# Hybrid attention/Hyena block: the filters' second small layer in fixed places among the first half's block cycles, and a late part's sums closed in one PSUM bank

## The chip, the cores and the metric

One core of one Trainium2 chip runs the whole kernel as one program. The metric is device time in microseconds for one execution. The kernel before was timed three times: 1696.48, 1691.30 and 1693.38 us, median 1693.38 us. A fourth execution was recorded by the hardware profiler: its own time is 1691.19 us and its span, from the first recorded instruction to the last, is 1689.4 us. All positions in time below are microseconds from the start of that span.

Engine names as the profile has them: PE is the matrix engine (matmuls and transposes), DVE the vector engine, ACT the scalar engine (activation functions, copies, casts), POOL the general engine, which here issues transfers, and SP the engine whose queue issues most loads. Each engine runs its own instructions in the order in which they stand.

## What is computed

One trunk layer over 1024 latent tokens and 256 context tokens of width 1024. Only the part that bears on the change is shown:

```
mod   = silu(c)     @ w_ada + b_ada        # 6 parts of 1024: shift1 scale1 gate1 shift2 scale2 gate2
mod_c = silu(c_ctx) @ w_ada + b_ada
h  = rmsnorm(x, norm1_g)   * (1 + scale1)  + shift1
hc = rmsnorm(ctx, norm1_g) * (1 + cscale1) + cshift1
k_c, v_c = split(hc @ w_in[:, 512:1536])
q, k, v, hv, hx1, hx2, gna, ghy = split(h @ w_in)

# Hyena filters: a small network of a position t, two sine layers of width 64
hid  = sin(freq * (features(t) @ w1 + b1))
hid  = sin(freq * (hid @ w2 + b2))
filt = (hid @ w3) * exp(-t * deltas)
```

After that come neighbourhood attention, a two-step long convolution with `filt`, a gated merge, and a SwiGLU feed-forward stage modulated by shift2, scale2 and gate2.

## The kernel before

**Tiles and stages.** Activations are kept with channels on the 128 partitions, so 1024 channels are 8 blocks (k = 0 to 7), and tokens run along the free axis in two halves of 512 (context: 256). A product of float32 accuracy is made of three fp32r matmuls: each operand is split into a high part (an ACT cast, line 177) and a low part (a DVE subtraction, line 178), and low x high, high x low and high x high are summed.

**The opening stage** is the one that the change touches, roughly the first 113 us of the span. `project` and its `opening` (line 792) multiply the normalized, modulated tokens by the value columns of `w_in`: for the first half of the tokens, then the second, then the context, and in each for k = 0 to 7. The operands of block k come from the generator `hidden`, which `opening` advances with `next(between)`. In the first half, block k's cycle also makes modulation block k + 1: eight small matmuls into a bank `ada_ps` (line 233), an ACT copy `msb`, four tiny matmuls that turn it into columns (line 244), two DVE operations that write `mod1` (lines 245 and 247); then ACT makes `htmp` from the transposed tokens `hT_ps` with it, casts it to `hTh`, and DVE makes `hTl`. In the second half and for the context the modulation is there already, and a cycle is: the transposes of block k + 2 on PE (line 261), `htmp` and `hTh` on ACT, `hTl` on DVE (`hcTh`, `hcTl` for the context), and then on PE eight matmuls that need `hTh` and a last four that need `hTl`.

**Side work in the opening.** Two more generators are advanced at fixed points of `hidden`:

- `filter_hidden` (`mlp`) makes the two sine layers. Each layer is two PE matmuls of 512 columns (line 453, bank `mlp_ps`), two DVE operations that add the bias and multiply by freq (line 454), five DVE operations of 1024 columns that bring the argument into the range of the sine (lines 455 to 463), and one ACT sine (line 465) that writes `feat` for the first layer and `hid` for the second. The sine needs a table of its own, which ACT loads ahead of it.
- `wide_sums` (`sums`) makes two late parts of the modulation, parts 3 and 4, by multiply-and-add on DVE: sixteen steps i = 0 to 15, each with one loaded row block `wal` of 128x1024 (line 1096 for the first step of a part, 1093 for the others). Step i issues load i + 3, so three loads are ahead. After the steps of a part `total` adds over the partitions with matmuls by a matrix of ones (line 1054, bank `ar_ps`) and DVE adds the sums to a row tile `arow` (line 1057).

**What sets the order.** Most instructions of this stage are pinned (`keep_in_program_order`): they stand on their engine as the generators produced them. Those that are not pinned are placed by the scheduler of the tile framework. Buffers come from pools: PSUM banks with the tag `f` (five of them) carry `ada_ps`, `hT_ps`, `mlp_ps` and `ar_ps` in turn; a ring of eight 128x1024 SBUF buffers carries in turn the raw weights, the x and context rows, the `wal` loads and the accumulator `aacc`. An instruction that writes a buffer waits until the last reader of its earlier content is done.

In the kernel before, the second sine layer is produced in the second half: its two matmuls on PE and its seven argument operations on DVE stand together in the cycle of block 6, after the closing of part 3. The sine itself stands on ACT ahead of `htmp` of block 7.

Of the kernel before, what the change touches and what calls it, by code (L numbers as in the profile page):

```python
# [10 lines left out]
F32 = mybir.dt.float32  # L11
F32R = mybir.dt.float32r
AF = mybir.ActivationFunctionType
ALU = mybir.AluOpType
# [4 lines left out]
P = 128  # L19
# [141 lines left out]
class Block:  # L161
# [121 lines left out]
    def hidden(self, pool, wpool, h1, mp, held, late, hT, hcT, psf):  # L283
# [30 lines left out]
        next(mlp)  # L314
# [26 lines left out]
        def split_weight(k):  # L341
            self.split(*(t[:, k % 2] for t in self.wv[k // 2]), raws[k], inorder)
# [13 lines left out]
        next(mlp)  # L356
# [8 lines left out]
        for k in range(8):  # L365
            h = pool.tile([P, 512], F32, tag="htmp", name="htmp", bufs=3)
# [3 lines left out]
            if k < 3:  # L370
                next(mlp)
# [5 lines left out]
            if k < 7:  # L377
                self.ada_cols_of(*ada, k + 1, sel)
                if 1 <= k + 1 <= 4:
                    block(k + 4)  # L380
                    if k in (0, 2):
                        weight(2 + k // 2)
                    for j in ((), (6, 7), (4,), (5,))[k]:
                        inorder(load(j))
                split_weight(k + 1)
                if 3 <= k:
                    square((6, 7, 4, 5)[k - 3], inorder)
                if k == 5:
                    xs.extend(ring("x") for _ in range(2))
                    for j in (8, 9):  # L390
                        inorder(load(j))
                    sums = self.wide_sums(ring, pool, psf)
                    next(sums)
                if k in (4, 6):
                    r = scaled(10 - k, 2, f"rstd1{k}", inorder)
                    for j in range(2):
                        times(xs[10 - k + j], r[:, j:j + 1], inorder)
# [6 lines left out]
        for k in range(8):  # L404
# [12 lines left out]
            if k in (1, 6):  # L417
                for _ in range(6 if k == 6 else 1):
                    next(mlp)
            if k == 6:  # L420
                after = [self.turned(psf, xs[8:], k, True) for k in range(2)]
# [3 lines left out]
        for k in range(8):  # L425
            if k:
                self.chunk(pool, after[k], 2, self.mod1[:, 1], *hcT, k, None, inorder, True)
            if k < 6:
                after.append(self.turned(psf, xs[8:], k + 2, True))
            if k in (0, 2, 4, 6):  # L430
                next(sums, None)
            yield

    def filter_hidden(self, pool, late, psf):
# [7 lines left out]
        for b in range(2):  # L442
            if b:
                hid, w3 = late()
                nc.sync.dma_start(w3, a["fw3"])
            w, src, dst = (w2, z, hid) if b else (w1, z[0:66], z)
            held = (lambda i: i) if b else pin
            arg = pool.tile([P, T], F32, tag="farg", name="farg", bufs=1)
            kf = pool.tile([P, T], F32, tag="fkf", name="fkf", bufs=1)
            for h in range(2):  # L450
# [3 lines left out]
                held(nc.vector.tensor_scalar(arg[:, sl], ps, col[:, b:b + 1], col[:, 2:3], op0=ALU.add, op1=ALU.mult))  # L454
            held(nc.vector.tensor_scalar(kf, arg, 1.0 / TWO_PI, MAGIC, op0=ALU.mult, op1=ALU.add))
            yield
            held(nc.vector.tensor_scalar(kf, kf, MAGIC, None, op0=ALU.subtract))
            yield
            held(nc.vector.scalar_tensor_tensor(arg, kf, -C1, arg, op0=ALU.mult, op1=ALU.add))
            yield  # L460
            held(nc.vector.scalar_tensor_tensor(arg, kf, -C2, arg, op0=ALU.mult, op1=ALU.add))
            yield
            held(nc.vector.tensor_scalar(arg, arg, PI_LO, -PI_LO, op0=ALU.min, op1=ALU.max))
            yield
            nc.scalar.activation(dst, arg, AF.Sin)
# [600 lines left out]
    def wide_sums(self, ring, pool, psf):  # L1066
# [15 lines left out]
        def total(part, acc):  # L1082
            for h in range(2):
                self.late_total(psf, r, ones, acc[:, 512 * h:512 * h + 512], part - 3, h, pin)
# [609 lines left out]
```

## Time and profile before

| | |
|---|---|
| median of three runs | 1693.38 us |
| profiled execution: own time | 1691.19 us |
| profiled execution: span | 1689.4 us |
| PE busy | 1647.0 us, 97% of the span |
| DVE busy | 1225.4 us, 73% |
| ACT busy | 697.8 us, 41% |
| mean granted PE clock | 0.992 |
| first-half cycle on PE (22.49 to 27.31) | 4.82 us |
| second-half cycle on PE (68.05 to 71.29) | 3.24 us |
| PE idle between 75 and 94 | 4.54 us and 5.99 us |

A row of a timeline gives the start, the length, the engine, the line, the operation with the tile that it writes and those that it reads, the shape and the count; in square brackets stands how long the engine was idle just before, and what ended that. For a load's line in the SP queue, the start is when the transfer was issued. A matmul in plain float32 shows as two records, so `x2` there is one matmul. Rows of a view by windows give, for a stretch of time, the busy time of each engine and, as PEclk, the share of full speed at which PE was clocked.

### The profile page before, as it was taken

Reading aid. Unit: us, or ns where it says so; the run is one execution under the profiler, and the core shown is the slowest. Engines: PE = TensorE matmul, PEld = TensorE weight load, DVE = VectorE, ACT = ScalarE, POOL = GpSimd, SP = SyncE. Lnnn points to the kernel's source line nnn. Section 1 sums busy time; section 2 is a strip of 40 time slices with the busy share of each in tenths; the row PEclk is TensorE's granted clock in tenths of the full one; section 3 lists DMA queues with packets and bytes.
Section 4 is the critical chain, followed back from the end, with each engine's and each line's share of the span. In section 5 each row is a group of like instructions: output and inputs, shape, how many; then the busy total and the mean of one; then the engine's idle time right before and its main releaser. Section 6 shows DMA issues by size and latency. Waiting matters only on the chain.

```text
span 1689.4 us, 22635 instructions
## 1 busy us (share of the span) xinstructions
PE 1647.0 (97%) x8138; PEld 1304.1 (77%) x8138; DVE 1225.4 (73%) x2071; ACT 697.8 (41%) x1216; POOL 148.6 (9%) x272
## 2 busy tenths in 40 slices
PE   8889999999999999999999999999999999999997
PEld 5667777777777788887887887888888888878886
DVE  4757899699999685556765868877865666389467
ACT  6453343312212146455653226633334333355455
POOL 1020000101000050111100001000100111000000
PEclk9999999999999999999999999999999999999999
DMA  9733555554555283445648314333432223395344
GB/s 361 256 133 128 184 174 189 190 173 161 181 201 194 93 265 126 130 122 161 191 157 279 123 63 175 131 129 121 150 106 94 100 103 116 115 384 162 100 120 155
DMA packets 108005, 274.37 MB, mean 162 GB/s; under 512 B 15215, under 2 KB 24307, under 8 KB 105589
## 3 DMA queue, kind: packets, MB, share of 16 engines
q1 hardware_dynamic: 87992, 212.39, 37.6%
q0 software_dynamic: 19104, 60.08, 10.5%
q8 instruction: 65, 1.06, 0.3%
q10 hardware_dynamic: 797, 0.45, 0.1%
q14 instruction: 47, 0.39, 0.1%
HBM read 205.48 MB, written 67.39 MB: 162 GB/s over the span
## 4 chain that ended last, share of the span: by engine, by line
PE 61%; DMA 3%; DVE 2%; issue 1%; ACT 1%; SPq 0%; DVEq 0%; ACTq 0%
PE x_ps L1393 15%; PE in_ps L199 9%; PE z_ps L1393 7%; PE out_ps L1331 5%; PE dx_ps L1562 5%; PE dz_ps L1562 3%; PE hy_ps L199 3%; PE y_ps L1393 2%; PE pt_ps L967 2%; PE pt_ps L953 2%; PE na_ps L199 2%; DMA w<-in_w 1%; PE s_ps L933 1%; PE dy_ps L1562 1%; DMA yhraw<-yh 1%
## 5 line engine op out<-in xcount | busy, mean ns | idle before, releaser
L199 PE MATMUL in_ps<-hTh,wl 128*128 128x512 f32 x576 | 233.0, 405 | 0.5 <-ACT proj L761 0.5
L199 PE MATMUL in_ps<-hTh,wh 128*128 128x512 f32 x576 | 227.3, 395 | 0.0
L199 PE MATMUL in_ps<-hTl,wh 128*128 128x512 f32 x576 | 226.3, 393 | 0.0
L199 PEld LDWEIGHTS in_ps<-hTh,wl 128*128 128x128 f32 x576 | 108.2, 188 | 26.4 <-issue 4.1
L199 PEld LDWEIGHTS in_ps<-hTh,wh 128*128 128x128 f32 x576 | 108.2, 188 | 23.9 <-issue 0.3
L199 PEld LDWEIGHTS in_ps<-hTl,wh 128*128 128x128 f32 x576 | 108.3, 188 | 21.8
L177 ACT CAST wh<-wr 128x1024 fp32r<-128x1024 f32 (+1 forms) x60 | 52.6, 877 | 140.9 <-PE in_ps L199 118.0
L178 DVE TENSOR_TENSOR wl<-wr,wh 128x1024 fp32r<-128x1024 f32 (+1 forms) x60 | 60.4, 1006 | 63.2 <-ACT wh L177 62.9
L178 DVE TENSOR_TENSOR ol<-ws,oh 128x512 fp32r<-128x512 f32 x88 | 60.4, 688 | 48.8 <-ACT oh L177 48.6
L178 DVE TENSOR_TENSOR ol<-ar,oh 128x512 fp32r<-128x512 f32 x77 | 52.8, 688 | 46.3 <-ACT oh L177 46.3
L177 ACT CAST oh<-ar 128x512 fp32r<-128x512 f32 x77 | 47.9, 622 | 83.2 <-PE dx_ps L1562 33.1
L177 ACT CAST oh<-ws 128x512 fp32r<-128x512 f32 x88 | 54.6, 622 | 58.2 <-PE x_ps L1393 26.4
L941 DVE CUSTOM_DVE_ANT_0 pe<-s_ps,bias 128x640 f32<-128x640 f32 x64 | 50.1, 820 | 31.8 <-PE s_ps L936 31.8
L942 ACT ACTIVATE pe<-pe,mx 128x640 f32<-128x640 f32 x64 | 52.6, 823 | 44.6 <-DVE mx L941 44.6
L1562 PE MATMUL dx_ps<-ol,oh 128*128 128x512 f32 x176 | 68.7, 390 | 1.7 <-DVE ol L178 1.7
L585 PE MATMUL dft_ps<-a,matf 128*128 128x512 f32 x128 | 66.8, 603 | 2.2 <-issue 2.0
L1562 PE MATMUL dx_ps<-oh,ol 128*128 128x512 f32 x176 | 67.4, 390 | 1.4 <-DVE ol L178 1.4
L1562 PE MATMUL dx_ps<-oh 128*128 128x512 f32 x176 | 68.5, 389 | 0.0
L177 ACT CAST oh<-wr 128x512 fp32r<-128x512 f32 x70 | 43.4, 622 | 52.0 <-PE x_ps L1393 16.0
L178 DVE TENSOR_TENSOR ol<-wr,oh 128x512 fp32r<-128x512 f32 x70 | 48.1, 689 | 22.0 <-ACT oh L177 21.9
L1333 DVE TENSOR_TENSOR x<-x,out_ps 128x512 f32<-128x512 f32 x64 | 42.8, 685 | 17.2 <-PE out_ps L1331 16.9
L1331 PE MATMUL out_ps<-wouh,ml 128*128 128x512 f32 x128 | 49.9, 390 | 0.0
(417 smaller groups left out, 4308.7 us busy)
## 6 DMA issues: line engine op xcount, KB each, us to landing
wr<-in_w SPq DMA_DIRECT2D x52, 512.0 KB, 3.5
ar<-g SPq DMA_DIRECT2D x77, 256.0 KB, 2.9
wr<-in_w_in SPq DMA_DIRECT2D x36, 512.0 KB, 3.9
matf<-in_dft_f SPq DMA_DIRECT2D x32, 384.0 KB, 3.3
bias<-in_rpb SPq DMA_DIRECT2D x64, 192.0 KB, 3.7
g<-t POOLq DMA_DIRECT2D x47, 256.0 KB, 3.0
w<-in_w SPq DMA_DIRECT2D x44, 256.0 KB, 5.4
x<-in_x SPq DMA_DIRECT2D x16, 512.0 KB, 6.5
```

What stands on the lines that cost most here:

```text
L177: pin(self.nc.scalar.copy(hi, src))
L178: pin(self.nc.vector.tensor_sub(lo, src, hi.bitcast(F32)))
L199: mm = nc.tensor.matmul(ps, ww[:, k * P:(k + 1) * P], xx[:, k, pos:pos + width], start=(i == 0), stop=(i == n - 1))
L585: nc.tensor.matmul(ps, m[:, 0], v.rearrange("p a b -> p (a b)"), start=True, stop=False)
L941: nc.vector.tensor_tensor_reduce(pe, ps[:, 256:896], bt, -1.0, 3e38, ALU.add, ALU.min, mx[:, 0:1])
L942: nc.scalar.activation(pe, pe, AF.Exp, bias=mx[:, 0:1], scale=-1.0, accum_out=mx[:, 1:2])
L953: pin(nc.tensor.transpose(pt[:, at:at + P], pe[:, c * P:(c + 1) * P], self.ident))
L967: pin(nc.tensor.matmul(pt[ch, 1280:1408], vv[:, ch], pts[:, hh, c * P:(c + 1) * P], start=(c == 0), stop=(c == 4), tile_position=(0, 64 * ...
L1331: nc.tensor.matmul(ps, gg[x][:, tk], ww[y][:, sl], start=(i == 0), stop=(i == n - 1))
L1333: nc.vector.tensor_add(x1[:, sl], x1[:, sl], ps)
L1393: mm = nc.tensor.matmul(ps, w[u][:, k * P:(k + 1) * P], x[v][:, k, :], start=(start and k == 0 and i == 0), stop=(stop and k == 3 and i == 2),
L1562: nc.tensor.matmul(ps[j], x[u][:, j * P:(j + 1) * P], w[v], start=(start and i == 0 and c == 0), stop=(stop and i == N - 1 and k == len(re ...
```

## The change

It has two parts. First, `filter_hidden` is cut into more steps (one for each instruction or nearly so), all its instructions are pinned, and `hidden` advances it at other points: the second layer's first matmul at the start of block 3 of the first half, its second at the start of block 4, the DVE operations one or two at a time behind `hTl` of blocks 3 to 7 of the first half, the load of `fw3` at block 6 of the second half, and the sine at block 1 of the context. The first layer's operations also move by up to one block. Second, `sums` starts two steps earlier (steps 0 and 1 at block 7 of the first half, so that all sixteen are produced by the end of the second half), and `total` puts its four matmuls into one bank, at partitions 0, 32, 64 and 96, with one DVE addition of 128x256 in the place of two banks and two additions of 64x256.

```diff
         mlp = self.filter_hidden(mp, late, psf)
-        next(mlp)
+        steps = lambda n: [next(mlp) for _ in range(n)]
+        steps(5)
...
-        next(mlp)
+        steps(1)
...
         for k in range(8):
+            if k in (3, 4):
+                steps(1)
             h = pool.tile([P, 512], F32, tag="htmp", name="htmp", bufs=3)
...
             self.split(*(t[:, k, :] for t in hT[0]), h, inorder)
-            if k < 3:
-                next(mlp)
+            steps((1, 2, 0, 1, 2, 2, 1, 1)[k])
+            if k == 7:
+                for _ in range(2):
+                    next(sums)
...
                 split_weight(k + 1)
+                if k == 1:
+                    steps(1)
...
-            if k in (1, 6):
-                for _ in range(6 if k == 6 else 1):
-                    next(mlp)
             if k == 6:
+                steps(1)
                 after = [self.turned(psf, xs[8:], k, True) for k in range(2)]
...
-            if k in (0, 2, 4, 6):
+            if k == 1:
+                steps(1)
+            if k in (2, 6):
                 next(sums, None)
...
-        for b in range(2):
-            if b:
-                hid, w3 = late()
-                nc.sync.dma_start(w3, a["fw3"])
-            w, src, dst = (w2, z, hid) if b else (w1, z[0:66], z)
-            held = (lambda i: i) if b else pin
+        for b, w, src in ((0, w1, z[0:66]), (1, w2, z)):
...
                 pin(nc.tensor.matmul(ps, w, src[:, sl], start=True, stop=True))
-                held(nc.vector.tensor_scalar(arg[:, sl], ps, col[:, b:b + 1], col[:, 2:3], op0=ALU.add, op1=ALU.mult))
-            held(nc.vector.tensor_scalar(kf, arg, 1.0 / TWO_PI, MAGIC, op0=ALU.mult, op1=ALU.add))
+                yield
+                pin(nc.vector.tensor_scalar(arg[:, sl], ps, col[:, b:b + 1], col[:, 2:3], op0=ALU.add, op1=ALU.mult))
+                yield
+            pin(nc.vector.tensor_scalar(kf, arg, 1.0 / TWO_PI, MAGIC, op0=ALU.mult, op1=ALU.add))
             yield
...
-            nc.scalar.activation(dst, arg, AF.Sin)
+            if b:
+                hid, w3 = late()
+                nc.sync.dma_start(w3, a["fw3"])
+                yield
+            pin(nc.scalar.activation(hid if b else z, arg, AF.Sin))
             yield
...
         def total(part, acc):
-            for h in range(2):
-                self.late_total(psf, r, ones, acc[:, 512 * h:512 * h + 512], part - 3, h, pin)
+            ps = psf.tile([P, 512], F32, tag="f", name="ar_ps")
+            for j in range(4):
+                pin(nc.tensor.matmul(ps[32 * j:32 * j + 32, 0:256], ones, acc[:, 256 * j:256 * j + 256], start=True,
+                                     stop=True, tile_position=(0, 32 * j)))
+            rs = r[:, 256 * (part - 3):256 * (part - 3) + 256]
+            pin(nc.vector.tensor_add(rs, ps[:, 0:256], rs))
```

How the order of the instructions moves, at the two places that the prediction rests on. On DVE, in the later blocks of the second half, the kernel before has this, from step 10 of the sums on (`arow` is the closing of part 3, `farg` and `fkf` are the second sine layer, the last row is the low part of block 7):

```order
L1093 SCALAR_TENSOR_TENSOR aacc<-wal,cs,aacc 128x1024
L1057 TENSOR_TENSOR arow<-ar_ps,arow 64x256
L1093 SCALAR_TENSOR_TENSOR aacc<-wal,cs,aacc 128x1024
L1057 TENSOR_TENSOR arow<-ar_ps,arow 64x256
L454 TENSOR_SCALAR farg<-mlp_ps,mlp 128x512 x2
L455 TENSOR_SCALAR fkf<-farg 128x1024
L457 TENSOR_SCALAR fkf<-fkf 128x1024
L459 SCALAR_TENSOR_TENSOR farg<-fkf,farg 128x1024
L461 SCALAR_TENSOR_TENSOR farg<-fkf,farg 128x1024
L463 TENSOR_SCALAR farg<-farg 128x1024
L178 TENSOR_TENSOR wl<-wr,wh 128x1024
L178 TENSOR_TENSOR hTl<-htmp,hTh 128x512
```

The changed kernel has this there, from the low part of block 4 on (the first L1108 is step 8; the last two rows are the low part of context block 0 and the evictions of the second half's banks):

```order
L178 TENSOR_TENSOR hTl<-htmp,hTh 128x512
L1108 TENSOR_SCALAR aacc<-wal,cs 128x1024
L1105 SCALAR_TENSOR_TENSOR aacc<-wal,cs,aacc 128x1024
L178 TENSOR_TENSOR hTl<-htmp,hTh 128x512
L1105 SCALAR_TENSOR_TENSOR aacc<-wal,cs,aacc 128x1024 x2
L1096 TENSOR_TENSOR arow<-ar_ps,arow 128x256
L178 TENSOR_TENSOR hTl<-htmp,hTh 128x512
L1105 SCALAR_TENSOR_TENSOR aacc<-wal,cs,aacc 128x1024 x2
L178 TENSOR_TENSOR hTl<-htmp,hTh 128x512
L1105 SCALAR_TENSOR_TENSOR aacc<-wal,cs,aacc 128x1024 x2
L178 TENSOR_TENSOR hcTl<-htmp,hcTh 128x256
L809 COPY vst<-in_ps 128x512 x2
```

The sine layer is gone from here, and steps 10 and 11 now stand ahead of the low part of block 6 (steps 8 and 9 did before), steps 12 and 13 ahead of that of block 7, and steps 14 and 15 ahead of the context's first low part.

On PE, the kernel before has this behind block 5 of the second half (the last row is block 6's first matmul):

```order
L792 MATMUL in_ps<-wh,hTl 128x512 x4
L1054 MATMUL ar_ps<-aacc,ones 32x256 x4
L453 MATMUL mlp_ps<-feat,mlp 128x512 x2
L261 MATMUL hT_ps<-ident,x 128x128 x4
L792 MATMUL in_ps<-wl,hTh 128x512
```

In the changed kernel a second-layer matmul stands in the first half, behind blocks 2 and 3, ahead of the next modulation block's matmuls; the first of the two places reads:

```order
L800 MATMUL in_ps<-wh,hTl 128x512 x4
L455 MATMUL mlp_ps<-feat,mlp 128x512
L233 MATMUL ada_ps<-wada,csp 32x256 x8
L261 MATMUL hT_ps<-ident,x 128x128 x4
L800 MATMUL in_ps<-wl,hTh 128x512
```

The four closing matmuls of part 3 (`ar_ps`) stand one block earlier, behind block 4's last four matmuls and ahead of the transposes of block 7. The second accumulator now takes the first one's buffer, so that step 8 of the sums waits for these four; loads 11 and 12 of the sums take the buffers of two x tiles and wait for the transposes of block 7 on them. From the end of the opening on, the instructions stand in the same order on every engine as before.

More of the change, by code (lines that the diff above doesn't have):

```diff
@@ L453, in filter_hidden @@
                 pin(nc.tensor.matmul(ps, w, src[:, sl], start=True, stop=True))
-                held(nc.vector.tensor_scalar(arg[:, sl], ps, col[:, b:b + 1], col[:, 2:3], op0=ALU.add, op1=ALU.mult))
-            held(nc.vector.tensor_scalar(kf, arg, 1.0 / TWO_PI, MAGIC, op0=ALU.mult, op1=ALU.add))
+                yield
+                pin(nc.vector.tensor_scalar(arg[:, sl], ps, col[:, b:b + 1], col[:, 2:3], op0=ALU.add, op1=ALU.mult))
+                yield
+            pin(nc.vector.tensor_scalar(kf, arg, 1.0 / TWO_PI, MAGIC, op0=ALU.mult, op1=ALU.add))
             yield
-            held(nc.vector.tensor_scalar(kf, kf, MAGIC, None, op0=ALU.subtract))
+            pin(nc.vector.tensor_scalar(kf, kf, MAGIC, None, op0=ALU.subtract))
             yield
-            held(nc.vector.scalar_tensor_tensor(arg, kf, -C1, arg, op0=ALU.mult, op1=ALU.add))
+            pin(nc.vector.scalar_tensor_tensor(arg, kf, -C1, arg, op0=ALU.mult, op1=ALU.add))
             yield
-            held(nc.vector.scalar_tensor_tensor(arg, kf, -C2, arg, op0=ALU.mult, op1=ALU.add))
+            pin(nc.vector.scalar_tensor_tensor(arg, kf, -C2, arg, op0=ALU.mult, op1=ALU.add))
             yield
-            held(nc.vector.tensor_scalar(arg, arg, PI_LO, -PI_LO, op0=ALU.min, op1=ALU.max))
+            pin(nc.vector.tensor_scalar(arg, arg, PI_LO, -PI_LO, op0=ALU.min, op1=ALU.max))
             yield
-            nc.scalar.activation(dst, arg, AF.Sin)
+            if b:
[3 more added lines that the diff above has]
+            pin(nc.scalar.activation(hid if b else z, arg, AF.Sin))
             yield
```

## The prediction, made before the changed kernel was run

> **What bounds the kernel now.** I read the page first, then PE's waits in the first 200 us, then the timelines of PE, DVE and ACT around those waits. The page and the waits:
>
> ```profile
> PE 1647.0 (97%) x8138; PEld 1304.1 (77%) x8138; DVE 1225.4 (73%) x2071; ACT 697.8 (41%) x1216; POOL 148.6 (9%) x272
> ```
>
> ```profile
> PE in_ps L792 <- ACT hTh L177: 6.3, 2, 6.0
> PE mlp_ps L453 <- DVE arow L1057: 4.5, 1, 4.5
> ```
>
> PE is the bound nearly everywhere, so time taken off its line early is kept unless something later gives it back. The two long waits (6.0 and 4.5 us) lie in the opening. PE there, with three rows of the first half ahead:
>
> ```profile
> 22.49 1.07 PE L233 MATMUL ada_ps<-wada,csp 128*32 128x256 f32 x16
> 23.49 0.66 PE L261 MATMUL hT_ps<-ident,x 128*128 128x128 f32 x4
> 27.31 1.07 PE L233 MATMUL ada_ps<-wada,csp 128*32 128x256 f32 x16
> ...
> 68.05 0.60 PE L261 MATMUL hT_ps<-ident,x 128*128 128x128 f32 x4
> 70.36 1.09 PE L792 MATMUL in_ps<-wh,hTl 128*128 128x512 f32 x4
> 71.29 0.60 PE L261 MATMUL hT_ps<-ident,x 128*128 128x128 f32 x4
> 71.64 0.48 PE L792 MATMUL in_ps<-wl,hTh 128*128 128x512 f32 x1
> 74.88 0.64 PE L1054 MATMUL ar_ps<-aacc,ones 128*32 128x256 f32 x8
> 75.45 1.12 PE L453 MATMUL mlp_ps<-feat,mlp 128*128 128x512 f32 x2
> 81.11 2.07 PE L453 MATMUL mlp_ps<-feat,mlp 128*128 128x512 f32 x2 [4.54 <-DVE arow L1057]
> 82.97 1.32 PE L261 MATMUL hT_ps<-ident,x 128*128 128x128 f32 x4
> 93.57 0.80 PE L792 MATMUL in_ps<-wl,hTh 128*128 128x512 f32 x1 [5.99 <-ACT hTh L177]
> 98.86 0.41 PE L261 MATMUL hT_ps<-ident,x 128*128 128x128 f32 x2
> 100.51 0.38 PE L261 MATMUL hT_ps<-ident,x 128*128 128x128 f32 x2
> ```
>
> The second mlp matmul waits for a bank that DVE's closing of part 3 (`arow`) frees, behind a late load; then the layer's argument and its sine hold block 7's `hTh`:
>
> ```profile
> 51.70 0.68 DVE L178 TENSOR_TENSOR hTl<-htmp,hTh 128x512 fp32r<-128x512 f32 x1
> 57.61 0.69 DVE L178 TENSOR_TENSOR hTl<-htmp,hTh 128x512 fp32r<-128x512 f32 x1 [1.20 <-ACT hTh L177]
> 58.22 0.75 DVE L1096 TENSOR_SCALAR aacc<-wal,cs 128x1024 f32<-128x1024 f32 x1
> 59.00 1.28 DVE L1093 SCALAR_TENSOR_TENSOR aacc<-wal,cs,aacc 128x1024 f32<-128x1024 f32 x1
> 60.80 1.28 DVE L1093 SCALAR_TENSOR_TENSOR aacc<-wal,cs,aacc 128x1024 f32<-128x1024 f32 x1
> 71.82 1.28 DVE L1093 SCALAR_TENSOR_TENSOR aacc<-wal,cs,aacc 128x1024 f32<-128x1024 f32 x1 [0.47 <-DMA wal<-in_w_ada]
> 79.44 1.29 DVE L1093 SCALAR_TENSOR_TENSOR aacc<-wal,cs,aacc 128x1024 f32<-128x1024 f32 x1 [2.32 <-DMA wal<-in_w_ada]
> 80.64 0.41 DVE L1057 TENSOR_TENSOR arow<-ar_ps,arow 64x256 f32<-64x256 f32 x1
> 80.98 1.27 DVE L1093 SCALAR_TENSOR_TENSOR aacc<-wal,cs,aacc 128x1024 f32<-128x1024 f32 x1
> 88.28 0.69 DVE L463 TENSOR_SCALAR farg<-farg 128x1024 f32<-128x1024 f32 x1
> ```
>
> ```profile
> 89.05 1.28 ACT L465 ACT_TABLE_LOAD   x1 [18.92 <-DVE farg L463]
> 90.34 1.06 ACT L465 ACTIVATE hid<-farg 128x1024 f32<-128x1024 f32 x1
> ```
>
> **What can go.** From 71.29 to 98.86 PE took 27.57 us. Without waits and at full clock that is a block of 3.24 (68.05 to 71.29), the closing 0.57 (74.88 to 75.45), another 3.24, and a block without transposes, 3.24 - 0.35 = 2.89: 9.94. So 17.6 us could go: both waits, both mlp matmuls, and slow matmuls behind each wait.
>
> **What the first half pays.** The two mlp matmuls go there, each bounded by 0.9 and 1.12 us (a matmul is two records of 512 columns, sixteen records of `ada_ps` take 1.00; the row itself is 1.12); I take 2.0 for both. Nothing covers them: PE is never idle there. DVE and ACT have room:
>
> ```profile
> 40.00:50.00 10.00, 10.00 (x72) 7.07 (x72) 5.63 (x14) 8.43 (x17) 0.00 (x0) 1.00 0.75 270
> 44.82 0.28 DVE L245 TENSOR_SCALAR mod<-ada_ps,bcol,ng 128x2 f32<-128x2 f32 x1 [0.92 <-PE ada_ps L244]
> ```
>
> The tightest place is the cycle with the scaling of x, whose 0.92 us of idle time must take a 0.69 and a 1.23: `mod1` comes 1.0 late, about what its `hTh` was ahead. I take nothing, at worst 0.5. The first layer's sine comes one cycle sooner on ACT at the same price, and `fw3` goes out one place later on SP, behind load 15, with the whole context part still ahead of its first reader: nothing for both, at worst the sine's 2.3 if ACT had no room. That leaves 17.6 - 2.0 = 15.6 as the most that the change can bring.
>
> **What is late next: the sums.** Two steps now stand ahead of each low part, one block earlier. Positions with the 2.0 added:
>
> - Steps 0 and 1 follow block 7's `hTl` (53.7) and an argument operation: 53.7 + 0.6 + 0.6 + 0.8 + 1.3 = 57.0 for the end of step 1, against 60.28 before. The DVE evictions behind them come late for PE by some 0.2.
> - Step 2 stands behind the second half's `hTl` of block 1, 57.61 + 2.0, so it starts at about 60.0, only 0.8 sooner. Steps 2 to 7 took 60.80 to 73.10; with loads 3 and 4 issued 3 us sooner I put the end of step 7 at 71. A scaling of x (0.7) and `hTl` of block 4 follow: 72.4. PE wants it at 70.36 + 2.2 = 72.6. No wait, by a hair.
> - Step 8 waits for PE's four closing matmuls: 72.6 + 0.93 + 0.57 = 74.1. Steps 8 and 9 and `hTl` of block 5 end at 76.8; PE wants it at 74.1 + 2.3 = 76.4. Wait 0.4 to 0.5.
> - Load 11 waits for the transposes at 74.3, with loads 12 to 15, `fw3` and the first weight behind it. The nearest row is load 10, which had as many behind it: issued 73.13, used 79.44.
>
> ```profile
> 73.13 0.80 SPq L1080 DMA_DIRECT2D wal<-in_w_ada  x2
> DMA to landing us min/median/max: 4.2/6.2/7.5
> ```
>
>   At 6.3 step 11 starts at 80.6 and ends at 81.9; `arow` (one addition, 0.41) and `hTl` of block 6 make it 82.7. PE wants it at 77.7 + 0.4 + 2.0 = 80.1: **wait 2.5**.
> - Steps 12 and 13 and `hTl` of block 7: 85.8 if loads 12 and 13 are there by 82.6 and 83.9, wanted at 85.6. Wait 0.2. PE ends the second half at 86.7.
> - Steps 14 and 15, the low part and the eviction that frees the context's second bank now stand in a row on DVE: 85.7 + 2.5 + 0.4 + 0.7 = 89.3; PE wants that bank at 87.4. **Wait 1.9.** The prices are those of the next rows.
>
> ```profile
> 97.29 0.42 DVE L178 TENSOR_TENSOR hcTl<-htmp,hcTh 128x256 fp32r<-128x256 f32 x1
> 98.24 0.69 DVE L801 COPY vst<-in_ps 128x512 f32<-128x512 f32 x1 [0.54 <-PE in_ps L792]
> ```
>
> - The sine (1.28 + 1.06 on ACT, ahead of context block 2's operand) and a weight cast behind it: 0.3, since the wait of 1.9 gave ACT that time. Uncovered, it costs the whole 2.3.
>
> Together 0.2 + 0.4 + 2.5 + 0.2 + 1.9 + 0.3 = 5.5. A second way to it: step 0 to step 11 (58.22 to 80.98) took 2.07 each, two of them 4.1 per block against PE's 3.24; over seven blocks 6.3, and 4.1 for the last two steps, less the 3.3 of lead: 7.1.
>
> **The clock.** Behind a wait, matmuls ran at half speed:
>
> ```profile
> 75.00:78.50 3.50, 1.57 (x10) 0.33 (x7) 1.89 (x2) 0.00 (x0) 0.00 (x0) 0.99 0.88 301
> 78.50:81.90 3.40, 0.79 (x1) 0.50 (x2) 2.46 (x3) 0.00 (x0) 0.56 (x2) 0.50 1.00 390
> ...
> 85.30:88.70 3.40, 2.28 (x10) 1.50 (x8) 3.30 (x4) 0.00 (x0) 0.00 (x0) 1.00 0.28 105
> ```
>
> ```profile
> 913.50 0.50 PE L199 MATMUL na_ps<-yah,wl 128*128 128x512 f32 x1 [2.41 <-DVE wl L178]
> ```
>
> ```profile
> 915.00:920.00 5.00, 5.00 (x17) 3.96 (x16) 3.77 (x6) 2.35 (x4) 0.00 (x0) 0.69 0.98 304
> ```
>
> A stretch with PE idle 55% of it was followed by half clock, as was a wait of 2.41 later in the kernel (0.69 on average over 5 us, some 3 us at half). So the wait of 2.5 probably brings it too: 1.7 us of matmul time, most of it in front of a wait that is there anyway. I take 0.6, between 0 and 1.7. The Trainium skill ("TensorE: Matmul & The Clock Gate", part 1) puts the drop behind an idle window of about 3.4 us and advises against gaps longer than that; by it the 2.5 would cost nothing and the result be 0.6 us lower. The row at 913.50 speaks against that reading.
>
> **Sum.** 17.6 - 2.0 - 5.5 - 0.6 = 9.5 us. Against the profiled execution's own time, 1691.19, that is 1681.7; the median of the runs, 1693.38, is 2.2 above it, so I forecast **1683.9 us**. The single addition itself (0.41 for twice 0.41, and a bank less) is in the chain above: 0.4 us per part.
>
> **Rivals.**
> 1. *The load queue holds more.* Seven loads stand within 5 us, so all share. At the row's maximum of 7.5 step 11 slips 1.2, and steps 12 and 13 no longer start back to back; with the clock's full 1.7 the waits grow by 3.5 to 5: gain 4.5 to 6, about 1688. For: five loads close together are those that took longest (79.44 ended a wait of 2.32). Against: step 10's load goes out alone now.
> 2. *Given back later.* The next stage starts on time, but its loads or DVE chain hold it, and PE waits there: 1692 to 1694. For: DVE is busy 73% over the whole, so stages with less room than the average must exist. Against: behind the opening every queue has the same order, so all of it moves forward together, and PE is at 97%. The price is whatever is given back, up to all of it.
> 3. *Slower: the sums set the pace of every block.* All low parts stand behind steps, and a step needs a buffer's turnaround. From step 0 at 54.9 sixteen steps and the row of low part and eviction end the context's first block at 54.9 + 16 x + 2; it ended at 100.51 before. From x = 2.7 us per step on the kernel is slower, at 3.0 by 5 us: 1698. It was 2.07.
> 4. *No new wait.* Loads land within 4.2 (the row's minimum): waits of 1 us remain, gain 14.6, about 1679.
>
> **Chances.** Forecast 0.70, rival 1 0.14, rival 2 0.08, rival 3 0.04, rival 4 0.04. The range 1678.5 to 1688.5 takes in rivals 1 and 4 and the bounds of the sum. This kernel's measurement can tell about 0.3%, 5 us: faster (below 1688.3) is the forecast, rival 4 and 0.10 of rival 1, 0.84; within 0.3% the rest of it and rival 2, 0.12; slower 0.04.
>
> **What would show it.** No mlp matmul and no wait on `arow` between 73 and 84; block 7's `hTh` on ACT right behind block 6's; a wait of PE on `hTl` of 2 to 3 us in block 6 and of 1 to 2 us at the context's first block, both ending in a DVE wait for `wal`; the first-half cycles with an mlp matmul at 5.7 to 5.9 instead of 4.82; the context's first block ending near 90 instead of 100.51. Wrong would be: a DVE or ACT wait in the first half over 0.5, a wait of PE in block 6 over 5, or a gain in the opening that the total does not show.

## The result and the profile after

The changed kernel takes **1683.63 us** (median of 4 runs, 1682.88 to 1685.22) against 1694.16 us before (4 runs, 1691.30 to 1696.48): a ratio of 0.994, 95% interval 0.9922 to 0.9957. The forecast was 1683.9. The profiled execution took 1682.88 us with a span of 1681.1, against 1691.19 and 1689.4 before: 8.3 us less.

PE is the bound as before, and both long waits of the opening are gone. From the page of the changed kernel, and from its table of PE's waits in the first 200 us (columns: what waited and for whom, us in total, times, longest):

```profile
PE 1644.0 (98%) x8138; PEld 1300.5 (77%) x8138; DVE 1223.7 (73%) x2069; ACT 697.8 (42%) x1216; POOL 149.3 (9%) x272
```

```profile
PE in_ps L800 <- DVE vst L809: 1.5, 1, 1.5
PE in_ps L800 <- DVE hTl L178: 1.1, 3, 0.5
...
PE in_ps L800 <- ACT hTh L177: 0.3, 1, 0.3
```

The 6.0 and 4.5 us of before are replaced by 1.5 us at the context's first block and three short waits for low parts. PE's timeline of the changed kernel shows the places: the two mlp matmuls in the first half, each followed by a block of `ada_ps`, then the three waits in blocks 4, 5 and 6, the context's wait, and the filters' first matmul.

```profile
23.56 1.07 PE L233 MATMUL ada_ps<-wada,csp 128*32 128x256 f32 x16
28.39 1.07 PE L233 MATMUL ada_ps<-wada,csp 128*32 128x256 f32 x16
33.13 1.02 PE L455 MATMUL mlp_ps<-feat,mlp 128*128 128x512 f32 x2
34.08 1.07 PE L233 MATMUL ada_ps<-wada,csp 128*32 128x256 f32 x16
...
73.98 1.20 PE L800 MATMUL in_ps<-wh,hTl 128*128 128x512 f32 x4 [0.32 <-DVE hTl L178]
78.55 1.20 PE L800 MATMUL in_ps<-wh,hTl 128*128 128x512 f32 x4 [0.34 <-DVE hTl L178]
82.52 1.20 PE L800 MATMUL in_ps<-wh,hTl 128*128 128x512 f32 x4 [0.45 <-DVE hTl L178]
89.08 0.50 PE L800 MATMUL in_ps<-wl,hcTh 128*128 128x512 f32 x1 [1.54 <-DVE vst L809]
102.31 2.00 PE L503 MATMUL filt_ps<-fw,hid 64*128 64x256 f32 x16
```

The same last row of the kernel before:

```profile
112.69 2.00 PE L495 MATMUL filt_ps<-fw,hid 64*128 64x256 f32 x16
```

So the opening is shorter by 112.69 - 102.31 = 10.4 us, where 9.5 were forecast. Behind it nothing is reordered, and in these two executions 2.1 of the 10.4 are lost again; the section on the prediction says where. What DVE does between is the view that the experiments turn on. From its timeline in the changed kernel, steps 5, 8 and 11 of the sums, and the two evictions of the context's first block:

```profile
67.52 1.29 DVE L1105 SCALAR_TENSOR_TENSOR aacc<-wal,cs,aacc 128x1024 f32<-128x1024 f32 x1 [2.30 <-DMA wal<-in_w_ada]
...
75.82 0.75 DVE L1108 TENSOR_SCALAR aacc<-wal,cs 128x1024 f32<-128x1024 f32 x1 [1.90 <-PE ar_ps L1093]
...
80.24 1.28 DVE L1105 SCALAR_TENSOR_TENSOR aacc<-wal,cs,aacc 128x1024 f32<-128x1024 f32 x1 [0.55 <-DMA wal<-in_w_ada]
...
88.34 1.28 DVE L809 COPY vst<-in_ps 128x512 f32<-128x512 f32 x2
```

### The profile page after: what moved, and what is told of

Same layout as the page of the kernel before. It is cut to its first block, busy times and chain, and to the rows that moved or that the text cites. A ratio compares the mean times of both kernels' runs of the same rounds, so it can differ in the third digit from the quotient of the medians.

```text
span 1681.1 us, 22633 instructions
## 1 busy us (share of the span) xinstructions
PE 1644.0 (98%) x8138; PEld 1300.5 (77%) x8138; DVE 1223.7 (73%) x2069; ACT 697.8 (42%) x1216; POOL 149.3 (9%) x272
## 4 chain that ended last, share of the span: by engine, by line
PE 75%; issue 12%; DMA 5%; DVE 4%; ACT 2%; POOL 1%; SPq 0%; ACTq 0%; POOLq 0%; DVEq 0%
PE x_ps L1405 15%; PE in_ps L199 14%; PE z_ps L1405 7%; PE out_ps L1343 5%; PE dx_ps L1574 5%; PE dz_ps L1574 3%; PE hy_ps L199 3%; PE dft_ps L593 3%; PE y_ps L1405 2%; PE pt_ps L961 2%; PE pt_ps L975 2%; PE na_ps L199 2%; PE in_ps L800 2%; PE dft_ps L595 1%; PE dft_ps L594 1%
```

## The experiments

All are timed against the kernel before in the same session. The medians of the changed kernel and of its better variants lie within a few us of each other, and the intervals overlap; what tells them apart is the moment at which the filters' first matmul (`filt_ps`) starts in their profiles. The table has both. "From 55" is the time from the eight transposes in front of the second half's first low part to `filt_ps`; it leaves out what an execution lost or won at its very start. In two kernels (only the layer moved, last two steps late) three matmuls of the next stage, 0.36 us, stand ahead of `filt_ps`, which stand behind it in the others.

| kernel | median us | ratio to before, 95% | filt_ps starts | from 55 |
|---|---|---|---|---|
| before (four sessions) | 1692.85 to 1694.16 | | 112.69 | 60.27 |
| the change | 1683.63 | 0.9922 to 0.9957 | 102.31 | 47.11 |
| the change, second session | 1680.92 | 0.9917 to 0.9944 | 102.15 | 46.60 |
| only the layer moved | 1682.53 | 0.9929 to 0.9953 | 101.67 | 47.35 |
| only the sums moved | 1692.94 | 0.9985 to 1.0009 | 110.27 | 57.72 |
| change, argument late | 1692.02 | 0.9977 to 0.9999 | 110.66 | 56.43 |
| change, two banks | 1685.06 | 0.9940 to 0.9967 | 102.89 | 47.42 |
| change, last two steps late | 1681.56 | 0.9923 to 0.9952 | 102.27 | 48.25 |
| the same, sine early | 1680.32 | 0.9898 to 0.9939 | 101.14 | 45.52 |
| change, loads four ahead | 1680.94 | 0.9906 to 0.9942 | 100.28 | 45.99 |
| three together | 1682.30 | 0.9917 to 0.9955 | 101.64 | 46.73 |
| three, one accumulator buffer | 1679.67 | 0.9912 to 0.9937 | 99.91 | 44.51 |

### Only the layer moved

The filters' second layer as in the change; the sums' start, places and closings as before:

```diff
-            if k == 7:
-                for _ in range(2):
-                    next(sums)
...
-            if k in (2, 6):
+            if k in (0, 2, 4, 6):
                 next(sums, None)
...
-            ps = psf.tile([P, 512], F32, tag="f", name="ar_ps")
...
+            for h in range(2):
+                self.late_total(psf, r, ones, acc[:, 512 * h:512 * h + 512], part - 3, h, pin)
```

> Only the layer moves: the filters' second layer goes into the first half as in the change, while the sums keep their old start (two steps per block from block 1 of the second half, the last two in the context part) and close in two banks with two additions. Theory (the gain is the two waits of 4.5 and 6.0 us and the half clock behind them, paid with two mlp matmuls of 0.85): both waits are gone, the low part of block 7 waits 1 to 3 us behind step 11 and its load, and the context's first block waits under 1 us, since steps 14 and 15 stand later; filt_ps starts near 103 to 105 and the time is 1684 to 1687. Rival (the earlier sums are what frees the banks): a wait of 3 us or more on an arow addition stays between 73 and 84 us, and the time is above 1688.

It ran in 1682.53 us (1682.28 to 1686.34), 0.9929 to 0.9953 of before: all of the gain, 1.5 us better than the theory's range (1684 to 1687), and `filt_ps` starts at 101.67, where it had 103 to 105. Its waits of PE:

```profile
PE in_ps L797 <- DVE hTl L178: 1.8, 2, 1.3
PE in_ps L797 <- DVE vst L806: 1.7, 1, 1.7
```

The 1.3 us behind step 11 are there as foreseen; the context's 1.7 were foreseen under 1, since steps 12 and 13 take the place there that 14 and 15 have in the change. No wait on an addition is left, so the rival falls: the earlier sums are not needed to free a bank.

### Only the sums moved

The kernel before with the sums two steps earlier and one addition per part:

```diff
             if k < 3:
                 next(mlp)
+            if k == 7:
+                for _ in range(2):
+                    next(sums)
...
-            if k in (0, 2, 4, 6):
+            if k in (2, 6):
                 next(sums, None)
...
```

> Only the sums move: two steps earlier and one addition per part, with the second layer in its old place in the second half. Theory: the wait of the second mlp matmul shrinks from 4.5 us to 1 to 3, because the addition that frees its bank comes with step 11 one block sooner; the wait for the operand behind the sine stays at 5 to 7 us, because the argument's chain on DVE now stands behind four more steps; filt_ps starts at 109 to 112 and the time is 1690 to 1694. Rival (the sums' move is most of the gain): below 1688.

1692.94 us, 0.9985 to 1.0009 of before: no difference. The waits of PE:

```profile
PE in_ps L795 <- ACT hTh L177: 5.9, 2, 5.6
...
PE hT_ps L261 <- DVE farg L457: 2.0, 1, 2.0
PE in_ps L795 <- DVE hTl L178: 0.7, 2, 0.4
```

The wait of the second mlp matmul is gone, and 2.0 us of it come back at the transposes behind it, which wait for the eviction of that matmul. The wait behind the sine stays (5.6 us), and with it the half clock. `filt_ps` starts 2.4 us sooner than before, which the total doesn't show. The time, the wait behind the sine and `filt_ps` lie where the theory had them; that the first wait would move to the transposes it didn't say.

### The argument and the sine back in the second half

The change, but of the layer only the two matmuls and their evictions stay in the first half:

```diff
-            steps((1, 2, 0, 1, 2, 2, 1, 1)[k])
+            steps((1, 2, 0, 1, 1, 0, 0, 0)[k])
...
             if k == 6:
-                steps(1)
+                steps(7)
...
-            if k == 1:
-                steps(1)
```

> The change, but only the layer's two matmuls, their evictions stay in the first half; its argument (five operations on DVE, 4.5 us) and the sine go back to block 6 of the second half, ahead of block 7's operand. Theory (what pays is the argument's and the sine's place, not the matmuls'): the argument stands behind steps 12 and 13 and ends near 89, the sine near 92, and block 7's hTh waits for both: a PE wait of 7 to 9 us with half clock behind it, filt_ps near 110 to 113, and 1690 to 1694, no better than before. Rival (the two waits are worth the same, and one of them is gone): 1687 to 1689.

1692.02 us, 0.9977 to 0.9999 of before: of the 10.4 us in the opening 2.0 are left (`filt_ps` at 110.66), though neither mlp matmul is in the second half. PE's timeline, block 7:

```profile
92.19 0.79 PE L798 MATMUL in_ps<-wl,hTh 128*128 128x512 f32 x1 [9.71 <-ACT hTh L177]
```

The two waits of before, 4.5 and 6.0 us, are one of 9.7, above the theory's 7 to 9. So they weren't two costs side by side: the layer's chain (matmul, eviction, five operations on DVE, table load and sine on ACT) ends at a time that DVE's queue sets, and block 7's operand stands behind it on ACT. The argument's last operation ended at 88.97 us in the kernel before, at 87.76 with only the sums moved and at 88.33 here, however early its matmuls had run. (Steps 12 and 13, 2.60 us on DVE, stand ahead of the argument here and not in the kernel before; the wait holds up to that much of them.) A matmul that starts sooner mostly lengthens the wait behind it. What pays is that the argument and the sine leave that place.

### Two banks for a closing

The change with the closings of before:

```diff
-            ps = psf.tile([P, 512], F32, tag="f", name="ar_ps")
...
-            pin(nc.vector.tensor_add(rs, ps[:, 0:256], rs))
+            for h in range(2):
+                self.late_total(psf, r, ones, acc[:, 512 * h:512 * h + 512], part - 3, h, pin)
```

> The change, but a part's sums are closed as before, in two banks with two additions. Theory: one addition of 0.4 us more on DVE per part ahead of a low part, so waits of PE longer by 0.4 to 0.8 in all: 1683.5 to 1685. Rival (the second bank is what counts): a wait of PE of over 1.5 us on an arow addition or on transposes, and 1686 or more.

1685.06 us, just above the theory's range, 0.994 to 0.9967 of before; `filt_ps` 0.6 us later than in the change, and 0.3 later counted from 55. Waits of PE:

```profile
PE in_ps L800 <- DVE hTl L178: 1.7, 2, 1.1
PE in_ps L800 <- DVE vst L809: 1.7, 1, 1.7
```

Waits for low parts and evictions are longer by 0.6 and 0.2 us. That fits the theory's 0.4 to 0.8; the time itself can't tell it from nothing.

### The last two steps behind the context's evictions

```diff
-                for _ in range(2):
+                for _ in range(2 if k < 7 else 0):
                     next(sums)
...
-            if k in (2, 6):
+            if k in (0, 1, 2, 6):
                 next(sums, None)
```

> The change, but the last two steps of the sums (14 and 15) stand behind the two evictions of the context's first block on DVE. Theory (the wait of 1.54 us there is DVE's two steps ahead of the eviction): the wait is gone, block 7's low part comes no later, filt_ps starts 1.3 to 1.9 us sooner than in the change, and the time is 1681.5 to 1682.7. Rival (the time lost there is taken up again by the next thing late, the weight cast or the sum's closing): a new wait of 1 us or more between 88 and 102 us, and no difference from the change.

1681.56 us lies in the theory's range, but its mechanism failed: `filt_ps` starts at 102.27, where it was (101.9 without the next stage's three matmuls ahead of it). The wait for the eviction is gone and another has come one block later (PE's timeline):

```profile
92.22 0.50 PE L800 MATMUL in_ps<-wl,hcTh 128*128 128x512 f32 x1 [1.06 <-ACT hcTh L177]
```

It is the operand of context block 2, behind the sine on ACT. This was the rival, though by neither of the causes that it named. DVE's and PE's timelines of this run show one thing more:

```profile
67.52 1.29 DVE L1105 SCALAR_TENSOR_TENSOR aacc<-wal,cs,aacc 128x1024 f32<-128x1024 f32 x1 [3.20 <-DMA wal<-in_w_ada]
```

```profile
54.02 1.04 PE L261 MATMUL hT_ps<-ident,x 128*128 128x128 f32 x8
...
73.98 1.20 PE L800 MATMUL in_ps<-wh,hTl 128*128 128x512 f32 x4 [1.01 <-DVE hTl L178]
78.55 1.19 PE L800 MATMUL in_ps<-wh,hTl 128*128 128x512 f32 x4 [0.34 <-DVE hTl L178]
```

The row at 54.02 stands at 55.20 in the change's profile: this execution was 1.18 us ahead there. At 67.52 DVE began step 5 at the same moment as in the change, having waited 3.20 us for its load instead of 2.30; and PE's rows at 73.98 and 78.55 have the same start in both. The lead was used up by waiting: the load of step 5 went out 1.2 us sooner than in the change (60.6 against 61.8) and landed no sooner. From issue to step 5 it took 6.9 us here, and 5.5 to 6.0 in the change, its second profile and the runs with the argument late, two banks and the sine early. So DVE does wait for loads there, but that a lead is lost is seen in this one execution only; "The change once more" has two in which it stayed.

### Loads four ahead

To give the sums a fourth buffer for loads, the accumulators take the layer's scratch tile, which is free by then:

```diff
...
+        load()
+        yield
         for i, (part, k) in enumerate(order):
...
-                acc = ring("aacc")
+                acc = total_in.tile([P, D], F32, tag="fkf", name="aacc", bufs=1)
...
-            if i + 3 < len(order):
+            if i + 4 < len(order):
                 load()
```

> The change, with the sums' loads four ahead of their steps in place of three; the buffer for it comes from the accumulators, which take the place of the layer's second scratch tile. Theory (from step 5 on it is the loads that pace DVE and so the low parts: step 5 began at 67.52 us in the change and at the same 67.52 us with the last two steps late, though DVE was there 0.9 us sooner): DVE's wait of 2.30 us ahead of step 5 falls under 1, PE's three waits for low parts (1.1 us in all) fall to 0.5 or less, filt_ps starts 0.7 to 1.7 us sooner than 102.31, and the time is 1681.5 to 1683. Rival (DVE's own work sets the pace): the waits of PE stay over 0.9 us and filt_ps starts within 0.4 us of 102.3.

1680.94 us, 0.9906 to 0.9942 of before, below the range. `filt_ps` starts at 100.28, 2.0 us sooner than in the change (1.1 counted from 55). DVE's wait ahead of step 6, the longest for a load that is left in the second half, and PE's waits:

```profile
66.33 1.28 DVE L1109 SCALAR_TENSOR_TENSOR aacc<-wal,cs,aacc 128x1024 f32<-128x1024 f32 x1 [0.44 <-DMA wal<-in_w_ada]
```

```profile
PE in_ps L802 <- DVE vst L811: 1.5, 1, 1.5
...
PE in_ps L802 <- DVE hTl L178: 0.3, 1, 0.3
```

2.30 us of load wait became 0.44, and PE's 1.1 for low parts 0.3. Three loads ahead did hold that stretch up. The context's 1.5 is untouched: that one is DVE's own work.

### The sine early

The last two steps late, as in the run above, and the sine on ACT behind the context's first operand:

```diff
             if k == 7:
                 self.chunk(pool, after[0], 2, self.mod1[:, 1], *hcT, 0, None, inorder, True)
+                steps(1)
...
-            if k == 1:
-                steps(1)
```

ACT's timeline of the change shows the idle stretch which that fills, and the table load that starts the sine behind it:

```profile
86.17 1.07 ACT L809 COPY vst<-in_ps 128x512 f32<-128x512 f32 x2 [5.15 <-PE in_ps L800]
...
88.17 1.28 ACT L473 ACT_TABLE_LOAD   x1
```

> The change with the last two steps late (as in that run), and the second layer's sine on ACT directly behind the context's first operand, where ACT sat idle for 5.15 us. Theory (with the last two steps late, the 1.54 us turned into 1.06 us behind the sine and 0.26 us of the sum's closing): the wait for hcTh is gone, no other over 0.5 us takes its place between 88 and 102 us, filt_ps starts 0.9 to 1.5 us sooner than 102.27, and the time is 1680 to 1681.3. Rival (loads or the weight cast pace that stretch): filt_ps starts within 0.4 us of 102.27.

1680.32 us, 0.9898 to 0.9939 of before; `filt_ps` at 101.14, 1.1 us sooner than with the last two steps late alone (0.4 of it those three matmuls), although this execution was 1.6 us later at the transposes (55.62 against 54.02). Waits of PE:

```profile
PE in_ps L799 <- DVE hTl L178: 1.1, 3, 0.4
...
PE ar_ps L1092 <- DVE aacc L1104: 0.3, 1, 0.3
```

No wait at the context's first blocks but 0.3 for the closing of part 4. The context's 1.5 went with both edits: DVE's steps out of the way of the eviction, and ACT's sine out of the way of the next operand. The first alone moved the wait by a block; the second alone wasn't run.

### All three, and an order that the scheduler chose

Loads four ahead, last two steps late, sine early, and the second part's sum in a tile of its own, so that step 8 needn't wait for PE's closing matmuls (the diff is against the run with four loads ahead):

```diff
-                acc = total_in.tile([P, D], F32, tag="fkf", name="aacc", bufs=1)
+                acc = (total_in if part == 3 else pool).tile([P, D], F32, tag="fkf" if part == 3 else "junk", name="aacc", bufs=1)
```

> Three things together on top of the change: loads four ahead, the last two steps and the sine as in the run with the early sine, and the second part's sum in a tile of its own, so that step 8 need not wait for PE (1.90 us of DVE). Theory (loads pace blocks 3 to 6, ACT and DVE the context's first blocks): PE's waits between 55 and 102 us come to less than 1 us (3.0 in the change), filt_ps starts 2.5 to 4 us sooner than 102.31 and the time is 1679 to 1681. Rival (the gain of the one is what the other has already taken): no better than 1681.5.

1682.30 us, no better than the change: the theory's range was missed. ACT's and PE's timelines and PE's windows (busy us of each engine, then granted clock, DMA share and GB/s):

```profile
84.80 1.04 ACT L177 CAST wh<-wr 128x1024 fp32r<-128x1024 f32 x1 [2.90 <-DMA wr<-in_w_in]
85.75 1.07 ACT L810 COPY vst<-in_ps 128x512 f32<-128x512 f32 x2
```

```profile
86.38 0.50 PE L801 MATMUL in_ps<-wl,hcTh 128*128 128x512 f32 x1 [1.86 <-ACT vst L810]
```

```profile
83.61:87.02 3.41, 1.55 (x8) 1.05 (x8) 2.48 (x3) 2.22 (x4) 0.96 (x2) 1.00 0.26 100
87.02:90.43 3.41, 3.41 (x11) 2.63 (x10) 2.67 (x4) 2.52 (x6) 1.22 (x3) 0.50 0.63 231
```

The waits for low parts are gone, and PE ends block 7 at 84.1, 2.5 us sooner than in the change. But the scheduler, which orders what isn't held in place, now put the cast of the next weight ahead of ACT's two evictions. That cast waits for a load until 84.80, so PE waits 1.86 us for its bank, and the 3.4 us behind run at half clock. To see whether only that order was at fault, the next kernel leaves out the second part's own tile (the line with the minus above stands again), and there the evictions are ahead of the cast.

> The run with three things together, without the second part's tile of its own: loads four ahead, the last two steps late, the sine early. In the three together ACT's order had changed: the cast of a weight whose load landed at 84.80 us stood ahead of the two evictions of the context's first block, and PE waited 1.86 us for them, with half clock behind. Here the evictions stand ahead of that cast again. Theory (only that order spoilt the sum of the parts): no wait of over 0.6 us between 80 and 100 us, filt_ps starts 1.5 to 2.5 us sooner than the 101.64 of the three together, and the time is 1678.5 to 1680.3. Rival (the parts take the same time twice): filt_ps not before 101 and 1680.5 or more.

1679.67 us (1678.31 to 1680.47), 0.9912 to 0.9937 of before; `filt_ps` at 99.91, 1.7 us sooner than with the three together. PE's waits:

```profile
PE in_ps L801 <- DVE hTl L178: 0.3, 1, 0.3
PE in_ps L801 <- ACT hTh L177: 0.3, 1, 0.3
PE ar_ps L1094 <- DVE aacc L1108: 0.3, 1, 0.3
```

So the parts do add up in the opening: 2.2 us against the change of the same session (102.15). In the medians that is 1680.92 against 1679.67, with ranges that overlap: seen in the profile, not shown in the time.

### The change once more

> The change as it is, once more, for a second profile of it. Open is whether the 2.5 us that were foreseen for block 6's low part stayed out because PE reached it later in that one execution (its matmuls reached full clock at 16.2 us, against 13.6 in the kernel before, and everything up to 55 us was 1.07 us later for it). Theory (loads pace this stretch, so a sooner PE only waits more): if full clock comes before 15 us, filt_ps still starts within 0.6 us of 102.31, and PE's waits between 55 and 92 us are 0.7 to 1.5 us longer than the 2.65 of the first profile. Rival (the slip was a loss of its own): filt_ps starts 0.8 us or more sooner, with the same waits. The time is 1682.5 to 1684.5.

1680.92 us (1677.94 to 1682.05), 0.9917 to 0.9944. The condition of the theory didn't occur: full clock came as late as in the first profile (nine `awake_ps` matmuls in 4.05 us again), so this run can't tell the two apart. `filt_ps` started at 102.15 and PE waited 0.6 us for low parts instead of 1.1.

Other runs bear on the question, and most of what they show speaks for the rival. With the argument late, DVE has the same steps and loads from step 0 up to block 6, and PE was 0.97 us sooner at the transposes (54.23 against 55.20). Step 5 then began 1.11 us sooner (66.41), and PE's last matmuls of blocks 4 and 6 started 1.12 and 1.23 us sooner, after waits of 0.53 and 0.35 us where the change has 0.32 and 0.45:

```profile
72.86 1.20 PE L798 MATMUL in_ps<-wh,hTl 128*128 128x512 f32 x4 [0.53 <-DVE hTl L178]
...
81.29 1.19 PE L798 MATMUL in_ps<-wh,hTl 128*128 128x512 f32 x4 [0.35 <-DVE hTl L178]
```

With only the sums moved PE was 2.65 us sooner at the transposes, and step 5 began 2.95 us sooner. The loads go out behind DVE's steps and PE's transposes, so they move with them. In the run with the last two steps late the lead was lost to a load that took longer. So a slip at the start is mostly a loss of its own.

## Why the prediction was right

The time was foreseen to 0.3 us, the gain in the opening to 0.9 (9.5 against 10.4). The first of these is closer than the kernel repeats: its second session gave 1680.92. That moving the second layer out of the second half pays was seen rightly; one term of the new waits was wrong by 2 us, and others made up for it. Term by term:

- **What can go (17.6).** Right. Neither wait is left, and no window of the second half shows less than full clock. The prediction names the two waits side by side; the run with the argument late showed that they hang together: it took away the first and got one wait of 9.7.
- **The two mlp matmuls (2.0).** Each makes its cycle 5.69 us (28.39 to 34.08) instead of 4.83 (23.56 to 28.39): 0.86, 1.7 for both, just under the lower bound of 0.9.
- **Cover on DVE and ACT in the first half (nothing).** Right: the cycles without an mlp matmul kept their 4.8, and the only wait there, 0.28, was in the kernel before too.
- **New waits (5.5).** Measured as lost time against full-speed blocks of 3.24: evictions in block 0 0.35 (0.2 foreseen), block 4 0.7 (0), block 5 0.7 (0.4), blocks 6 and 7 together 0.95 (2.7), the context 1.8 (1.9), the sine nothing (0.3). Together 4.5. All but block 4 and block 6 are right to 0.3. **The term that failed is block 6's "wait 2.5"**: 0.45. Its price came from load 10 of the kernel before, 6.3 us from issue to use. In the changed kernel load 11 went out at 76.0 and landed 4.1 us later (a view of the loads at 76.0 and 76.4, the first landing soonest):

```profile
L1088 SPq DMA_DIRECT2D wal<-in_w_ada x2: 327/375/423, 76.0 to 76.4; - x2
...
DMA to landing us min/median/max: 4.1/4.7/5.2
```

  In six more runs with this order of the sums it took 3.7 to 4.1, which is rival 4's figure. Counted from the transposes that free the load's buffer (74.3 forecast, 75.68 measured), the low part was forecast after 8.4 us and was there after 6.8; PE was to come for it after 5.8 us and came after 6.4, having lost more in block 5. So some 1.6 us of the difference are the load and 0.6 PE. That step 11 began at 80.24, near the 80.6 of the forecast, is luck: its load went out later and took less. Load 10 of the kernel before followed another load by 1.8 us, load 11 here by 3.3; whether that is the reason wasn't tried.
- **The context's wait (1.9)** came at its price, but not from a load, as the prediction's signs had it: DVE worked without a break from 81.45 us to the end of the evictions at 89.62.
- **Loads (rival 1).** It had 0.14. Load 11 took 4.1 us and not its 7.5, so it didn't come. But DVE did wait 2.30 us for another load, ahead of step 5: with four loads ahead, `filt_ps` starts 1.1 us sooner counted from 55.
- **The clock (0.6).** Nothing: the waits stayed under 1.6 us. In the run of the three together a wait of 1.86, shorter than the 2.5 that the term was for, did bring 3.4 us of half clock. So the term stood on a right reading. The Trainium skill ("TensorE: Matmul & The Clock Gate", part 1), which puts the drop behind an idle window of about 3.4 us, doesn't agree with that row: the window ahead of the drop had PE busy for 1.55 of its 3.41 us.
- **Not in the sum: the start.** PE's first stretch took 1.07 us longer in the profile of the change: the row of `ada_ps` at 23.56 stands at 22.49 before. The matmuls that wake PE up ran at half speed for longer, though they began sooner. Here are their rows, of before and then of the change:

```profile
11.63 3.08 PE L359 MATMUL awake_ps<-csp 128*32 128x256 f32 x9
14.57 1.21 PE L233 MATMUL ada_ps<-wada,csp 128*32 128x256 f32 x13
```

```profile
11.32 4.05 PE L360 MATMUL awake_ps<-csp 128*32 128x256 f32 x9
15.17 1.75 PE L233 MATMUL ada_ps<-wada,csp 128*32 128x256 f32 x13
```

The change isn't the cause: the kernels with the same opening show 3.3 us (four loads ahead, last two steps late) as well as 4.05 (sine early, the change again). It differs from execution to execution.

Sum: 17.6 - 1.7 - 4.5 - 1.1 = 10.3, the measured 10.4. The forecast's 9.5 was close because errors met: the blocks 6 and 7 (1.75 too much), the clock (0.6), the sine and the matmuls (0.3 each) on one side, and on the other the start (1.1), which the prediction didn't have, and blocks 4, 5 and 0 (0.7, 0.3 and 0.15 too little). That they nearly cancel is luck.

**Given back later (rival 2).** In the two profiled executions 2.1 of the 10.4 us are lost behind the opening. The largest pieces are a longer wait at 621 us (the row of before, then of the change), and at 1470 a wait of 2.6 us in the place of 1.2 with half clock behind it, where the execution before kept full clock:

```profile
630.17 0.50 PE L199 MATMUL in_ps<-hTh,wl 128*128 128x512 f32 x1 [0.55 <-ACT proj L761]
```

```profile
621.56 0.51 PE L199 MATMUL in_ps<-hTh,wl 128*128 128x512 f32 x1 [2.06 <-ACT proj L769]
```

```profile
1466.88:1470.29 3.41, 0.79 (x4) 0.35 (x3) 0.83 (x2) 1.33 (x3) 0.00 (x0) 1.00 0.93 349
1470.29:1473.70 3.41, 3.40 (x8) 2.73 (x9) 3.41 (x6) 3.13 (x6) 0.00 (x0) 0.50 1.06 399
```

Elsewhere it is the other way round: around 915 us the kernel before fell to half clock and the changed one didn't. Both losses differ from execution to execution: in the second profile of the change the first wait is 0.55 again, and the clock stays full at 1470. The medians are 10.5 us apart in the first session and 11.9 in the second, the opening 10.4: no sign that the kernel gives anything back.

**Sums as the pace of every block (rival 3).** The bound was 2.7 us per step. From step 0 (55.76) to the end of step 15 (88.10) the change took 32.3, 2.0 per step: far from it.

**What the parts are worth.** The layer's move alone brings the whole gain (1682.53); the sums' move alone nothing (1692.94), and on top of the layer's move nothing that can be measured (47.11 against 47.35 from 55, and the latter holds the next stage's three matmuls). The lead of two steps ends in DVE's waits of 2.30 for a load and 1.90 for PE. The prediction had no term for the parts and so said nothing wrong here, but its reader would have credited the sums.

## What to carry to other kernels

Two waits can hang on one chain over several engines: before adding their prices, ask what the second would be if the first were gone, and move the whole chain, not its first instruction. The time of a load from issue to landing isn't a constant to be carried over either: load 11 took 4.1 us where load 10 of the kernel before had taken 6.2. Price a wait for a load as a range, count it from the event that lets the load go out, and look for the buffer that lets it go out sooner. And a small edit can let a scheduler reorder work that is not held in place: an eviction that landed behind a cast with a late load cost 1.9 us and then the clock.

## What the runs showed of the hardware

The granted clock changes on a grid of 3.41 us: in each of the twelve profiles the stretches between two changes are whole multiples of it. What goes with a drop is how busy PE was within one window of the grid. A window with PE busy for 1.55 of 3.41 us (the three together) was followed by half clock. One with 1.75 of 3.41 (only the layer moved, a wait of 1.66) was followed by full clock:

```profile
85.75:89.16 3.41, 1.75 (x9) 1.08 (x8) 3.38 (x5) 3.35 (x5) 1.91 (x4) 1.00 1.02 407
89.16:92.57 3.41, 3.41 (x20) 2.66 (x18) 3.25 (x5) 3.35 (x8) 0.28 (x1) 1.00 0.62 244
```

But that is no threshold. Over all windows at full clock of the twelve profiles, each with PE busy for less than 1.4 us was followed by half clock and none with more than 2.05; between these it goes either way (1.43 us kept full clock in the three together, 2.00 us near 1036 with four loads ahead did not), so the busy time alone doesn't decide there, and what else does wasn't tried. So a wait of 1.5 to 1.9 us may cost nothing or half a window, 1.7 us of matmul time: the waits of 1.54 in the change and 1.66 with only the layer moved cost none, the 1.86 of the three together did. The two profiles of the change had two and three windows at half clock between the opening and the end. The slip of 1 us at the start fits the same grid (PE wakes up sooner or later against it), but the record of the clock begins only at the first full clock (16.2 us in the change, 13.6 before), so this is argued, not shown.
